# Halved projections, eight square buffers and kept weights in a Conformer convolution stage

## The chip, the cores and the metric

The kernel runs on one core of one Trainium2 chip. A core has a matrix engine (TensorE, PE in the profile, with its weight loads listed apart as PEld), VectorE (DVE), ScalarE (ACT), GpSimd (POOL) and SyncE (SP), whose queue issues nearly all DMA transfers here. Each engine works through its own queue in order; the order on each is fixed when the program is built. The metric is the device time of one launch in microseconds; smaller is better.

## The reference

One inference step of a small streaming encoder with 1024 channels: 640 frames in all, 512 of a new stream (the prompt) and 8 running streams with 16 new frames each (the sample). Layer 0 is a Conformer convolution module followed by a SwiGLU FFN, layer 1 is chunked attention with an FFN. Only the convolution module is touched:

```python
def conv_module(h, hist, g, w_pw1, b_pw1, w_dw, b_dw, ln_g, ln_b, w_pw2, b_pw2):
    a, gate = jnp.split(rms_norm(h, g) @ w_pw1 + b_pw1, 2, axis=-1)
    glu = a * jax.nn.sigmoid(gate)
    full = jnp.concatenate([hist.astype(glu.dtype), glu], axis=1)
    y = lax.conv_general_dilated(
        full, w_dw[:, None, :].astype(full.dtype), window_strides=(1,), padding="VALID",
        dimension_numbers=("NWC", "WIO", "NWC"), feature_group_count=D_MODEL) + b_dw
    y = jax.nn.silu(layer_norm(y, ln_g, ln_b))
    return h + y @ w_pw2 + b_pw2, full[:, -CONV_HIST:]
```

So: a norm, a projection to 2 x 1024 channels, a gate, a causal convolution over 31 frames in each channel, a layer norm over the channels of each frame, silu, and a second projection that is added to the residual. Everything is float32.

## The kernel before, in words

Channels lie on the 128 partitions, in 8 blocks (0 to 7); frames lie along the free dimension, in two groups of 320 (group 0: the 128 sample frames and 192 of the prompt; group 1: the other 320). A float32 product is made of three passes of a rounded format: weights and activations are split into a high and a low part (`whi`, `wlo`, `xh`, `xl`), and `mm3` (lines 164 to 166) issues hi*hi, lo*hi and hi*lo. `wsplit` loads a weight tile of 1 MB into `raw` (SP queue, line 133), ScalarE makes `whi` (line 144) and VectorE `wlo` (line 148); each of the three tags has two buffers, so a tile can be split only when the one two before it is done with.

The stage is written as a list of steps, PLAN, which `step` works through in that order. A scheduler with a model of each engine's time then fixes the order on each engine; the place in the program is the priority, and blocks marked `high_priority` are moved ahead. For channel block c the steps are:

- `a`, `b`, `c`, `C`: the first projection and gate of block c. One group (`glu_`) takes two products of 24 matmuls, each in its own PSUM buffer (tag `mm`, four buffers that go round); ScalarE reads the gate with a tanh (line 582) and the linear half (line 585) into t tiles, VectorE multiplies them into `gall`, the row of history and new frames (lines 589, 595). `C` does both groups and also prepares the convolution on TensorE: `conv_load` expands the taps into `w4` on GpSimd (line 641), `conv_shift` writes the row to DRAM (`sa` for the sample and group 0, `sb` for group 1, line 650) and reads it back four times shifted (`xa`, `xb`, two buffers each, line 656). `D` (not in the plan before) is `C` with a row of the sample frames alone.
- `S`, `A`, `B`: the convolution of block c on TensorE (`conv_pe`, line 674): sample frames, the prompt frames of group 0, group 1. They use PSUM buffers of the same tag `mm`, and ScalarE copies the result into `y` (line 602).
- `d`: the convolution on VectorE, tap by tap (`conv`, line 623); `dp1s0` is the prompt of block 1 and the sample of block 0, and so on. `q`: the prompt's convolution of a block on GpSimd: ScalarE multiplies a tap (`cvt`, line 633, four buffers), GpSimd adds it to `ca` (line 636), 31 times; at the end ScalarE copies `ca` to `y`.
- `L7`: the late read of block 7's `xb`. `s`: the convolution state goes out.
- `n0`, `n1`: `conv_ln`, the layer norm of a group. `colmean` sums over channels: the first `cut` pieces are added up on GpSimd (`acc`, line 190), and what is left goes to TensorE as matmuls with a single column of ones (line 199), one for each piece and each of three tiles of frames. The mean is spread over the partitions (line 211), VectorE subtracts it (line 688), ScalarE squares (line 171), the squares are summed likewise (`rstd_bc`), GpSimd takes the root's inverse (line 239), VectorE multiplies (line 694), ScalarE does silu (line 696) and the split follows (lines 153, 154).
- `w0`, `w1`: `pw2`, the second projection of a group, in four weight tiles `m2` (48 matmuls a tile and group); VectorE adds the result to `h` (line 714).

The FFN follows, on the same engines: it computes the statistics of the first 320 frames, then of the second, and its first matmuls (line 361) need the normalised first half. PSUM tiles of tag `w2` (two buffers) hold the statistics and VectorE's convolutions.

Of the kernel before, what the change touches and what calls it, by code (L numbers as in the profile page):

```python
# [15 lines left out]
P = 128  # L16
D = 1024
# [24 lines left out]
HP = 2000  # L42
CUT, LCUT = 8, 6
PO = {2: 0, 4: 1}
PL1 = (0, 2, 0, 0, 0, 0, 0, 0)
PL2 = (0, 0)
SQ = 'aaaaaaaa'
C01 = 4
# [24 lines left out]
def tile_trunk(ctx, tc, xT, vecs, hist, w_pw1, w_pw2, w_in0, w_out0, w_in1, w_out1,  # L73
# [93 lines left out]

    def square(s, n, eng="a"):
        q = tp.tile([P, tw[0]], F32, tag="sq", name=nm("sq"))
        if eng == "a":  # L170
            nc.scalar.activation(out=q[:, :n], in_=s, func=AF.Square)
# [54 lines left out]
    def rstd_bc(pieces, n, engs=SQ, cut=CUT, r2=None, eng=nc.gpsimd, newton=False,  # L226
                accp=None):
# [451 lines left out]
    def conv_ln(g):  # L679
        n = gr[g][1]  # L680
        mu = w2t()
        order = LNO[g]
        r, v = colmean(mu, [lambda c=c: y[g][:, c, :] for c in order], n, LCUT if g else 0, "mst")
        if v is not r:
            nc.vector.tensor_copy(r[:, :len(tiles(n))], v)
        spread(mu, r, n)
        for c in order:
            nc.vector.tensor_tensor(out=y[g][:, c, :], in0=y[g][:, c, :], in1=mu[:, :n],
                                    op=ALU.subtract)
        bc, _ = rstd_bc([y[g][:, c, :] for c in order], n, SQ, 1)  # L690
        z = new_xs(g)
        for c in range(KT):
            yc = y[g][:, c, :]
            nc.vector.tensor_tensor(out=yc, in0=yc, in1=bc, op=ALU.mult)
            s = tp.tile([P, tw[0]], F32, tag="n1", name=nm("n1"), bufs=NB1)
            nc.scalar.activation(out=s[:, :n], in_=yc, func=AF.Silu, scale=col(V_LNG, c),
                                 bias=col(V_LNB, c))
            xsplit(s[:, :n], z[0][:, c, :], z[1][:, c, :])
# [20 lines left out]
    def step(op, arg):  # L719
# [13 lines left out]
        elif op == "x":  # L733
            def mid():
                xs[1] = rms(1, V_NCONV, SSQ1, 8, hold=w4t)
            glu(1, 0, *pws[1], mid=mid)
        elif op in "DC":
            load_hist(c, c + 1)
            w4 = conv_load(c)
            pws[c + 1] = wsplit(w_pw1[c + 1] if c + 1 < KT else w_pw2[0], 16, P)  # L740
            glu_(c, 0, *pws[c], None)
            xa = conv_shift(c, "a", 0, NXA if op == "C" else NSC)
            nc.sync.dma_start(convs_out[:, c], gs[:, c])
            glu(c, 1, *pws[c])
            x4s[c] = w4, xa, op == "C" and conv_shift(c, "b", NSC + HA, NXB, c == KT - 1)
        elif op == "d":
# [3 lines left out]
        elif op == "L":  # L750
            x4s[c] = x4s[c][:2] + (x4s[c][2](),)
        elif op in "SAB":
# [451 lines left out]
```

## Time and profile before

| | before |
|---|---|
| time, median of 3 runs | 1572.77 us (1565.56 to 1572.9) |
| the profiled execution's own time | 1570.35 us |
| its span, first to last instruction | 1568.3 us |
| granted TensorE clock, mean | 0.971 |
| TensorE busy | 1503.2 us, 96% |
| VectorE, ScalarE, GpSimd busy | 1004.9, 674.7, 213.4 us |
| DMA | 164.30 MB, mean 105 GB/s |

The convolution stage takes the first 292 us of the span; the rest is FFN, attention, FFN. In the profile a line such as `L199 PE MATMUL w<-onec,sq` reads: line 199 of the kernel, engine, operation, output tile from input tiles. A timeline row begins with start and duration in us; consecutive rows of one kind are merged, and their number stands behind an x. A window row begins with the stretch, its length, and the busy time of each engine with the number of instructions. The chain of work that ended last is followed back from the last instruction, at each step to what released it.

### The profile page before, as it was taken

The numbers are of one execution on the slowest core, as the hardware profiler recorded it, in microseconds if no ns is written. First come the engines' busy times: TensorE is split into PE (matmuls) and PEld (weight loads), VectorE is DVE, ScalarE is ACT, GpSimd is POOL, SyncE is SP. The second block draws the span as 40 slices with busy tenths as digits, with TensorE's granted clock in tenths as the row PEclk, the third lists the DMA queues.
The fourth block names the chain that finished last, engine by engine and source line by source line (L and its number), as shares of the span: only waits on it lengthen the run. The fifth ranks groups of instructions, "written<-read, shape, count | busy, mean of one in ns | idle before, by whom it ended". The sixth has DMA issues, their size and how long they took to land.

```text
span 1568.3 us, 27283 instructions
## 1 busy us (share of the span) xinstructions
PE 1503.2 (96%) x11186; PEld 1428.8 (91%) x11186; DVE 1004.9 (64%) x1997; ACT 674.7 (43%) x1295; POOL 213.4 (14%) x239
## 2 busy tenths in 40 slices
PE   5999799999999999999999999988999999999997
PEld 5998579999999999999988788866999999999996
DVE  5788435785675575558676667563685575575555
ACT  4665145454254244246654344442444254244233
POOL 5789001000000000004221111011000000000001
PEclk9999679999999999999999999997999999999998
DMA  7256303312213222223555554351112222222211
GB/s 231 72 150 174 82 20 108 135 48 88 81 61 101 81 74 88 82 81 114 194 179 169 170 182 165 125 196 57 55 48 88 81 70 92 81 74 88 81 54 68
DMA packets 55884, 164.30 MB, mean 105 GB/s; under 512 B 10064, under 2 KB 24528, under 8 KB 47056
## 3 DMA queue, kind: packets, MB, share of 16 engines
q1 hardware_dynamic: 55472, 162.26, 32.2%
q8 instruction: 88, 1.44, 0.4%
q10 hardware_dynamic: 288, 0.31, 0.1%
q14 instruction: 36, 0.29, 0.1%
HBM read 151.13 MB, written 11.42 MB: 104 GB/s over the span
## 4 chain that ended last, share of the span: by engine, by line
PE 83%; POOL 5%; DVE 4%; ACT 3%; DMA 2%; issue 2%; POOLq 0%; SPq 0%; DVEq 0%; ACTq 0%
PE mm L361 35%; PE mm L164 13%; PE mm L166 12%; PE mm L165 12%; POOL ca L636 5%; PE w L199 2%; PE mm L674 2%; PE w L1001 1%; PE am L986 1%; PE am L1032 1%; PE am L969 1%; DMA cache<-in_ck 1%; ACT whi L144 1%; PE w L945 1%; PE w L946 1%
## 5 line engine op out<-in xcount | busy, mean ns | idle before, releaser
L361 PE MATMUL mm<-XH,wlo 128*128 128x320 f32 x736 | 228.3, 311 | 0.4 <-DVE wlo L319 0.4
L361 PE MATMUL mm<-XH,whi 128*128 128x320 f32 x736 | 227.4, 311 | 0.0
L361 PE MATMUL mm<-XL,whi 128*128 128x320 f32 x736 | 225.4, 309 | 0.0
L164 PE MATMUL mm<-xh,whi 128*128 128x320 f32 (+2 forms) x640 | 203.2, 320 | 5.9 <-ACT xh L153 4.2
L165 PE MATMUL mm<-xh,wlo 128*128 128x320 f32 (+2 forms) x640 | 202.0, 316 | 0.6 <-DVE wlo L148 0.6
L166 PE MATMUL mm<-xl,whi 128*128 128x320 f32 (+2 forms) x640 | 199.8, 316 | 0.0
L165 PE MATMUL mm<-hid,wlo 128*128 128x320 f32 (+2 forms) x560 | 171.8, 308 | 0.0
L166 PE MATMUL mm<-hid,whi 128*128 128x320 f32 (+2 forms) x560 | 169.7, 308 | 0.0
L164 PE MATMUL mm<-hid,whi 128*128 128x320 f32 (+2 forms) x560 | 167.7, 308 | 0.0
L318 ACT ACTIVATE whi<-raw 128x1536 fp32r<-128x1536 f32 (+2 forms) x90 | 101.0, 1148 | 121.3 <-PE mm L166 89.2
L319 DVE TENSOR_TENSOR wlo<-raw,whi 128x1536 fp32r<-128x1536 f32 (+2 forms) x90 | 118.7, 1340 | 40.6 <-ACT whi L318 40.4
L361 PEld LDWEIGHTS mm<-XH,wlo 128*128 128x128 f32 x736 | 139.2, 189 | 0.8 <-DVE wlo L319 0.8
L361 PEld LDWEIGHTS mm<-XH,whi 128*128 128x128 f32 x736 | 138.8, 189 | 0.0
L361 PEld LDWEIGHTS mm<-XL,whi 128*128 128x128 f32 x736 | 137.9, 188 | 0.0
L164 PEld LDWEIGHTS mm<-xh,whi 128*128 128x128 f32 x640 | 123.3, 193 | 9.9 <-ACT xh L153 4.9
L165 PEld LDWEIGHTS mm<-xh,wlo 128*128 128x128 f32 x640 | 123.6, 193 | 1.2 <-DVE wlo L148 0.8
L166 PEld LDWEIGHTS mm<-xl,whi 128*128 128x128 f32 x640 | 123.2, 194 | 1.2 <-issue 1.0
L361 PE MATMUL mm<-XH,vhi 128*128 128x320 f32 x368 | 114.2, 310 | 1.9 <-ACT XH L445 1.9
L361 PE MATMUL mm<-XH,vlo 128*128 128x320 f32 x368 | 113.8, 309 | 0.0
L361 PE MATMUL mm<-XL,vhi 128*128 128x320 f32 x368 | 113.1, 308 | 0.2
L165 PEld LDWEIGHTS mm<-hid,wlo 128*128 128x128 f32 x560 | 105.1, 188 | 0.0
L166 PEld LDWEIGHTS mm<-hid,whi 128*128 128x128 f32 x560 | 104.7, 188 | 0.0
(210 smaller groups left out, 3404.4 us busy)
## 6 DMA issues: line engine op xcount, KB each, us to landing
raw<-in_w_in SPq DMA_DIRECT2D x38, 1024.0 KB
cache<-in_ck SPq DMA_DIRECT2D x32, 512.0 KB
cache<-in_cv SPq DMA_DIRECT2D x32, 512.0 KB
raw<-in_w_pw SPq DMA_DIRECT2D x14, 1024.0 KB
raw<-in_w_out SPq DMA_DIRECT2D x18, 768.0 KB
raw<-in_w_kq SPq DMA_DIRECT2D x8, 1024.0 KB
raw<-in_w_in SPq DMA_DIRECT2D x12, 512.0 KB
raw<-in_w_out SPq DMA_DIRECT2D x12, 384.0 KB
```

The source lines that it names most:

```text
L144: nc.scalar.activation(out=hi[:, a:b], in_=raw[:, a:b], func=AF.Copy)
L164: nc.tensor.matmul(ps, wh, xh, start=(i == 0), stop=False)
L165: nc.tensor.matmul(ps, wl, xh, start=False, stop=False)
L166: nc.tensor.matmul(ps, wh, xl, start=False, stop=(i == last))
L199: nc.tensor.matmul(st[:, 512 + t * w + k:513 + t * w + k], s[:, a:a + P], onec, start=True, stop=True)
L318: nc.scalar.activation(out=hi[:, a:b], in_=src, func=AF.Copy)
L319: nc.vector.tensor_tensor(out=lo[:, a:b], in0=src, in1=hi[:, a:b].bitcast(F32), op=ALU.subtract)
L361: nc.tensor.matmul(pt, wt, v[x][:, k, :], start=(first and k == i == 0), stop=(k == 3 and i == 2), skip_group_check=True)
L636: nc.gpsimd.tensor_tensor(out=acc, in0=acc, in1=pr, op=ALU.add)
L674: nc.tensor.matmul(pt[32 * q:32 * q + 32, 0:n], w4[0:r, 4 * tg + q, :], mv, start=(tg == 0), stop=(tg == 7))
L945: nc.tensor.matmul(ps, QQ[:, q], KK[:, 0:n], start=True, stop=False)
L946: nc.tensor.matmul(ps, QQ[:, q], KL[:, 0:n], start=False, stop=True)
```

## The change

The plan is rewritten, and four smaller things are changed.

1. Steps `E` and `F` are new: `E` is the group 0 half of `C` (history, taps, next weights, products, the `sa`/`xa` transfers), `F` the group 1 half (products, `sb`/`xb`). Blocks 6 and 7 use them, with convolutions between: `E6 S4 A4 F6 B4 E7 S5 A5 F7 S6 A6`, where before stood `S4 A4 B4 C6 S5 A5 C7 S6 A6`.
2. Block 3 uses `D`, so its sample convolution is on TensorE (`S3`); VectorE's last convolution is `ds2` instead of `ds2s3`.
3. Group 0's mean has its first five pieces added on GpSimd (before: none), group 1's five (before six), in other orders. The squares are written to a tile with eight places, at the place of the low part of group 1's activations, where before two buffers went round. Group 1's squares are all added on GpSimd (before: none), group 0's none, as before.
4. The multiply, silu and split of group 0 have high priority, and silu writes to the four `cvt` buffers where before it had two of its own.
5. The second projection of group 1 takes the weight tiles in the order 2, 3, 0, 1 and uses tiles 2 and 3 as group 0 left them, without loading and splitting them again.

```diff
-CUT, LCUT = 8, 6
+CUT, LCUT, SQCUT = 8, (5, 5), (1, 8)
...
+M2 = ((0, 1, 2, 3), (2, 3, 0, 1))
...
-LNO = ((0, 1, 4, 2, 5, 3, 6, 7), (0, 1, 4, 2, 5, 3, 6, 7))
-PLAN = ("a0 y x1 b0 b1 q0 dp1s0 c2 ds1p2 c3 C4 q3 ds2s3 C5 S4 A4 B4 C6 S5 A5 C7 S6 A6 S7 A7 n0 B5 L7 B6 "
-        "B7 s0 n1 w0 w1")
+LNO = ((0, 1, 4, 5, 6, 2, 3, 7), (0, 1, 4, 2, 3, 5, 6, 7))
+PLAN = ("a0 y x1 b0 b1 q0 dp1s0 c2 ds1p2 D3 C4 S3 q3 ds2 C5 E6 S4 A4 F6 B4 E7 S5 A5 F7 S6 A6 S7 "
+        "A7 n0 B5 L7 B6 B7 s0 n1 w0 w1")
...
-    def square(s, n, eng="a"):
-        q = tp.tile([P, tw[0]], F32, tag="sq", name=nm("sq"))
+    def square(s, n, eng="a", q=None):
+        if q is None:
+            q = tp.tile([P, tw[0]], F32, tag="sq", name=nm("sq"))
...
-        r, v = colmean(st, [lambda s=s, e=e: square(s, n, e) for s, e in zip(pieces, engs)], n,
+        r, v = colmean(st, [lambda s=s, e=e, i=i: square(s, n, e, sqs if sqs is None else sqs[:, i, :])
+                         for i, (s, e) in enumerate(zip(pieces, engs))], n,
                        cut, "rst", eng, accp)
...
-        r, v = colmean(mu, [lambda c=c: y[g][:, c, :] for c in order], n, LCUT if g else 0, "mst")
+        r, v = colmean(mu, [lambda c=c: y[g][:, c, :] for c in order], n, LCUT[g], "mst")
...
-        bc, _ = rstd_bc([y[g][:, c, :] for c in order], n, SQ, 1)
+        sq = xp.tile([P, KT, n], F32, tag="xl1", name=nm("sql"))
+        bc, _ = rstd_bc([y[g][:, c, :] for c in order], n, SQ, SQCUT[g], sqs=sq)
         z = new_xs(g)
-        for c in range(KT):
...
-            s = tp.tile([P, tw[0]], F32, tag="n1", name=nm("n1"), bufs=NB1)
...
+        with tc.high_priority(offset=HP * (1 - g)):
+            for c in range(KT):
...
+                s = cp.tile([P, T], F32, tag="cvt", name=nm("cvt"), bufs=CVT)[:, :n]
...
     def pw2(g, z):
         n = gr[g][1]
-        for m2 in range(KT // 2):
-            if g == m2 == 0:
-                wh, wl = pws[KT]
-            else:
-                wh, wl = wsplit(w_pw2[m2], 16, P, pool=PL2[g])
+        for m2 in M2[g]:
+            if (KT, m2) not in pws:
+                pws[KT, m2] = wsplit(w_pw2[m2], 16, P, pool=PL2[g])
+            wh, wl = pws[KT, m2]
+            if m2 < 2:
+                del pws[KT, m2]
...
-        elif op in "DC":
-            load_hist(c, c + 1)
-            w4 = conv_load(c)
-            pws[c + 1] = wsplit(w_pw1[c + 1] if c + 1 < KT else w_pw2[0], 16, P)
-            glu_(c, 0, *pws[c], None)
-            xa = conv_shift(c, "a", 0, NXA if op == "C" else NSC)
-            nc.sync.dma_start(convs_out[:, c], gs[:, c])
-            glu(c, 1, *pws[c])
-            x4s[c] = w4, xa, op == "C" and conv_shift(c, "b", NSC + HA, NXB, c == KT - 1)
+        elif op in "CDEF":
+            if op != "F":
+                load_hist(c, c + 1)
+                w4 = conv_load(c)
+                if c + 1 < KT:
+                    pws[c + 1] = wsplit(w_pw1[c + 1], 16, P)
+                else:
+                    pws[KT, 0] = wsplit(w_pw2[0], 16, P)
+                glu_(c, 0, *pws[c], None)
+                x4s[c] = [w4, conv_shift(c, "a", 0, NSC if op == "D" else NXA), None]
+                nc.sync.dma_start(convs_out[:, c], gs[:, c])
+            if op != "E":
+                glu(c, 1, *pws[c])
+                if op != "D":
+                    x4s[c][2] = conv_shift(c, "b", NSC + HA, NXB, c == KT - 1)
```

More of the change, by code (lines that the diff above doesn't have):

```diff
@@ L226, in rstd_bc @@
     def rstd_bc(pieces, n, engs=SQ, cut=CUT, r2=None, eng=nc.gpsimd, newton=False,
-                accp=None):
+                accp=None, sqs=None):
         st = w2t()
         nt = len(tiles(n))
-        r, v = colmean(st, [lambda s=s, e=e: square(s, n, e) for s, e in zip(pieces, engs)], n,
+        r, v = colmean(st, [lambda s=s, e=e, i=i: square(s, n, e, sqs if sqs is None else sqs[:, i, :])
+                         for i, (s, e) in enumerate(zip(pieces, engs))], n,
                        cut, "rst", eng, accp)
@@ L689, in conv_ln @@
                                     op=ALU.subtract)
-        bc, _ = rstd_bc([y[g][:, c, :] for c in order], n, SQ, 1)
+        sq = xp.tile([P, KT, n], F32, tag="xl1", name=nm("sql"))
+        bc, _ = rstd_bc([y[g][:, c, :] for c in order], n, SQ, SQCUT[g], sqs=sq)
         z = new_xs(g)
-        for c in range(KT):
-            yc = y[g][:, c, :]
-            nc.vector.tensor_tensor(out=yc, in0=yc, in1=bc, op=ALU.mult)
-            s = tp.tile([P, tw[0]], F32, tag="n1", name=nm("n1"), bufs=NB1)
-            nc.scalar.activation(out=s[:, :n], in_=yc, func=AF.Silu, scale=col(V_LNG, c),
-                                 bias=col(V_LNB, c))
-            xsplit(s[:, :n], z[0][:, c, :], z[1][:, c, :])
+        with tc.high_priority(offset=HP * (1 - g)):
+            for c in range(KT):
+                yc = y[g][:, c, :]
+                nc.vector.tensor_tensor(out=yc, in0=yc, in1=bc, op=ALU.mult)
+                s = cp.tile([P, T], F32, tag="cvt", name=nm("cvt"), bufs=CVT)[:, :n]
+                nc.scalar.activation(out=s, in_=yc, func=AF.Silu, scale=col(V_LNG, c),
+                                     bias=col(V_LNB, c))
+                xsplit(s, z[0][:, c, :], z[1][:, c, :])
         return z
@@ L750, in step @@
         elif op == "L":
-            x4s[c] = x4s[c][:2] + (x4s[c][2](),)
+            x4s[c][2] = x4s[c][2]()
         elif op in "SAB":
```

## The prediction

> **What bounds the kernel now.** I read the page first, then the chain of work that ended last, then windows of busy time around the one place where the clock row dips, then the timelines of TensorE, ScalarE, VectorE and GpSimd there.
>
> ```profile
> PE 1503.2 (96%) x11186; PEld 1428.8 (91%) x11186; DVE 1004.9 (64%) x1997; ACT 674.7 (43%) x1295; POOL 213.4 (14%) x239
> ...
> PEclk9999679999999999999999999997999999999998
> ```
>
> TensorE is busy 96% of the span, so only its idle time, its slow time and its useless work can be saved. The clock row has one deep dip, slices 5 and 6 (157 to 235 us): the end of the convolutions and the layer norms. The windows of that stretch (columns: PE, PEld, DVE, ACT, POOL busy with counts, granted clock, DMA share, GB/s):
>
> ```profile
> 155.50:161.20 5.70, 4.82 (x129) 3.71 (x128) 3.79 (x12) 4.22 (x8) 1.41 (x2) 1.00 0.49 192
> 161.20:178.30 17.10, 6.73 (x128) 5.25 (x128) 12.46 (x31) 1.36 (x5) 0.00 (x0) 0.70 0.81 150
> 178.30:195.00 16.70, 16.66 (x103) 11.11 (x103) 0.35 (x2) 0.00 (x0) 0.00 (x0) 0.59 0.00 1
> 195.00:216.90 21.90, 20.38 (x223) 13.98 (x222) 6.04 (x18) 8.07 (x16) 2.59 (x3) 1.00 0.15 35
> 216.90:239.30 22.40, 21.69 (x92) 21.43 (x93) 8.68 (x20) 9.87 (x22) 0.00 (x0) 0.54 0.00 1
> 239.30:292.40 53.10, 53.10 (x372) 52.93 (x370) 34.45 (x49) 29.63 (x42) 8.04 (x7) 1.00 0.41 140
> 292.40:301.10 8.70, 5.83 (x31) 5.31 (x30) 8.56 (x16) 5.64 (x9) 0.00 (x0) 0.80 0.41 130
> ```
>
> Two kinds of loss: 10.4 us idle in the second window (17.10 - 6.73), and 56 us at a clock of 0.54 to 0.70. The chain names the idle:
>
> ```profile
> 157.22 0.45 ACT y L602
> 157.67 0.42 ACT t L582
> ...
> 158.88 2.73 DMA sa<-gall
> ...
> 162.99 6.49 DMA xa<-sa
> 169.94 6.73 PE mm L674 x128
> 176.67 1.67 issue
> ```
>
> The tanh of channel block 7 (t) runs only at 157.67, behind y<-ca, the end of GpSimd's convolution q3; from it a round trip through DRAM takes until 162.99 + 6.49 = 169.48, and S7, A7 start then. The slow time comes from the statistics, matmuls that stream one column (L199). Prices at both clocks, from TensorE's timeline (an fp32 matmul of these shows as two records; start, us, count):
>
> ```profile
> 109.67 4.56 PE L674 MATMUL mm<-xa,w 128*32 128x128 f32 x128
> 114.05 4.50 PE L674 MATMUL mm<-xb,w 128*32 128x320 f32 x64
> ...
> 155.55 1.96 PE L674 MATMUL mm<-xa,w 128*32 128x128 f32 x64
> ...
> 183.01 6.56 PE L199 MATMUL w<-onec,y 128*128 128x1 f32 x30
> ...
> 199.20 1.50 PE L199 MATMUL w<-onec,sq 128*128 128x1 f32 x12
> ...
> 219.04 4.00 PE L199 MATMUL w<-onec,sq 128*128 128x1 f32 x18 [0.66 <-ACT sq L171]
> ```
>
> and of the chain, the products:
>
> ```profile
> 223.52 0.27 PE mm L164
> ...
> 309.24 66.73 PE mm L361 x455
> ```
>
> So a statistics record costs 0.125 us warm (1.50/12) and 0.22 us at half clock (6.56/30, 4.00/18); a product matmul 0.147 us warm (66.73/455; the same 128x320 shape) and 0.27 at half clock; S+A 4.56, B 4.50, S alone 1.96 us warm.
>
> **The change part by part.**
>
> *E/F halves.* Before, C6, S5 A5, C7, S6 A6 stood between; now E7, S5 A5, F7, S6 A6. Behind E7's products TensorE has S5 A5 4.56 + F7's 48 x 0.147 = 7.0 + S6 A6 4.56 = 16.2 us of work, before 11.6. The trip from t to landed xa took 169.48 - 157.67 = 11.8 us, which fits if t runs at once. It won't: ScalarE's queue is paced by GpSimd (y<-ca waits 4.02 us for it; below, the two timelines).
>
> ```profile
> 152.37 0.55 ACT L585 ACTIVATE t<-mm,hb 128x320 f32<-128x320 f32 x1
> 156.94 0.72 ACT L602 ACTIVATE y<-ca 128x192 f32<-128x192 f32 x2 [4.02 <-POOL ca L636]
> 157.58 0.51 ACT L582 ACTIVATE t<-mm,hb 128x320 f32<-128x320 f32 x1
> ```
>
> ```profile
> 130.07 1.92 POOL L641 TENSOR_TENSOR w<-i,dwv 128x1024 f32<-128x1024 f32 x1
> ```
>
> In the written order E7's second product comes earlier by S5 A5 (4.6) and later by the new S3 (2.0): 2.6 us. Its neighbour, the linear half (L585, at 152.37, one product or 3.5 us earlier), already stands ahead of y<-ca, so t most likely moves ahead too, to about 152.4, plus 1.9 us because q3 gets one more tap expansion (L641: D3 uses a third early buffer) on GpSimd. xa then lands at 154.3 + 11.8 = 166; TensorE reaches S7 at 161 + 2.0 + 1.5 (stalls, below) = 164.5. The wait is 0 to 9 us; I take 3: **-6**. With a short wait the clock holds and S7 A7 take 4.56 instead of 6.73: **-2**.
>
> *What each moved step issues.* E6/E7 issue history, taps, the next weights, the sa/xa transfers and convs; F6/F7 sb/xb. SP is in order: xb6 waits for B4 (buffer), xa7 for A5, and the next raw weights stand behind; by the order above both are done some 5 and 10 us before SP gets there. In PSUM (four buffers) F6/F7 now want E6's and E7's banks after S, A and one product (4.6 + 3.5 = 8.1 us), where before A5 wanted C6's second bank after 7.0 + 1.96 = 9.0 us and stalled 0.70:
>
> ```profile
> 137.18 2.81 PE L674 MATMUL mm<-xa,w 128*32 128x192 f32 x64 [0.70 <-ACT t L582]
> ```
>
> Three such places, each at worst as late as t is now: 0 to 6, **+1.5**.
>
> *D3, S3, ds2.* S3 adds 64 records to TensorE, **+2**. VectorE loses 31 of its 62 sample taps, which run till 174.6:
>
> ```profile
> 167.97 6.62 DVE L623 SCALAR_TENSOR_TENSOR w<-gall,dwv,w 128x128 f32<-128x128 f32 x17
> ```
>
> They held y[0][2] and y[0][3], and with them part of the 1.67 us gap behind A7: **-1** (0 to -1.7).
>
> *Statistics.* The windows of that line alone:
>
> ```profile
> 178.30:195.00 16.70, 8.73 (x48) 8.56 (x48) 0.59 0.00 1
> ...
> 216.90:239.30 22.40, 9.10 (x42) 9.37 (x42) 0.54 0.00 1
> ```
>
> Group 0's mean: 8 pieces x 3 tiles = 48 records become 24 (four adds on GpSimd, in front of the last pieces 2, 3, 7): 8.7 us at half clock become 3.0 warm or 5.3 slow, **-5**. Group 1's mean: cut 6 to 5, 18 to 24 records, **+0.7**.
>
> *B5 in the slow stretch.* The 54 conv records of 178 to 195 us took 16.7 - 8.7 = 8.0 us; warm they are 54 x 0.070 = 3.8. If the clock holds -4.2, else 0: **-3.5**.
>
> *Squares.* Group 0 keeps 48 records. Group 1 had those 42 of 216.9 to 239.3 and 6 behind; now 6 in all, since GpSimd adds all eight: **-9**. The other 50 records of that window are products, 42 of them slow: 42 x 0.12 = **-5** when nothing sparse stands between them, and the 0.66 us idle goes, **-0.7**. These products stayed slow although TensorE was busy 21.69 of 22.40 us, and the clock rose at 239.3, behind the last block but one of statistics: I take the sparse blocks for the cause. The Trainium skill, TensorE: Matmul & The Clock Gate, Part 1, has the clock halved after an idle window of about 3.4 us and full again after one busy window of that length. If every busy record counts as activity there, the products should have been warm by about 224, and this -5 would be some -1, a time of 1552; the trace disagrees, unless one-column matmuls don't count.
>
> *What is late next.* Group 1's chain: squares, seven GpSimd adds, z. The groups of 216.95 to 292.5 us (count, busy, mean ns, idle before), and an add of the window before:
>
> ```profile
> L148 DVE TENSOR_TENSOR wlo<-raw,whi 128x2048 fp32r<-128x2048 f32 x6 | 13.7, 2291 | 6.5 <-ACT whi L144 6.4
> ...
> L144 ACT ACTIVATE whi<-raw 128x2048 fp32r<-128x2048 f32 x6 | 11.4, 1904 | 6.2 <-PE mm L166 6.2
> ...
> L696 ACT ACTIVATE n<-y,vec 128x320 f32<-128x320 f32 x14 | 9.0, 646 | 6.0 <-DVE xl L154 3.3 <-DVE y L694 2.8
> ...
> L153 ACT ACTIVATE xh<-n 128x320 fp32r<-128x320 f32 x15 | 6.9, 463 | 0.3
> ...
> L190 POOL TENSOR_TENSOR acc<-acc,sq 128x320 f32<-128x320 f32 x4 | 5.3, 1317 | 2.2 <-ACT sq L171 2.0
> ...
> L171 ACT ACTIVATE sq<-y 128x320 f32<-128x320 f32 x8 | 3.7, 466 | 8.1 <-PE w L199 6.8 <-DVE y L688 1.3
> ...
> L239 POOL TENSOR_TENSOR rst<-rst,mhalf 128x3 f32<-128x3 f32 x2 | 1.9, 946 | 32.6 <-DVE rst L232 32.6
> ```
>
> ```profile
> L190 POOL TENSOR_TENSOR acc<-acc,y 128x320 f32<-128x320 f32 x3 | 2.6, 869 | 41.0 <-ACT y L602 40.9
> ```
>
> z of group 0 now goes first on ScalarE, 8 x (0.65 + 0.46) = 8.9 us, then 3.7 of squares; the adds, 7 x 1.32 = 9.2 at worst, run beside them and end a little later: some 13.5 us after the second projection begins. Root and spread about 3, then z of group 1, 9 us alone and 16 with weight splits between: ready 25 to 32 us in. Group 0's products cover 192 x 0.147 = 28.2, and the last piece is needed 3 us later. A stall of 0 to 4, **+2**.
>
> *Kept weights.* Two loads fewer, 2 x 1.9 us of ScalarE and 2 x 2.3 of VectorE, in a window where TensorE is busy 53.10 of 53.10: nothing. But group 1 now ends on rows 0 to 3, which the FFN's second-half squares add first, so three or four links follow the last row; ScalarE and VectorE carry them while they build the FFN's first operands, for which TensorE already idles 2.9 of 8.7 us (the last window): 0 to 4, **+1.5**. Eight square buffers, four silu buffers and the priority of z cost nothing by themselves; the squares' tile is that of xs[1], last read by F7, 9 us of convolutions earlier.
>
> Sum: -6 -2 +1.5 +2 -1 -5 +0.7 -3.5 -9 -5 -0.7 +2 +1.5 = -24.5. Against the profiled execution, 1570.35, that is 1545.9; the median of the runs, 1572.77, is 2.4 above it, so I say 1548. With every term at its good end it is about -35 (1538), with every one at its bad end +3 (1575).
>
> **The rivals.**
>
> *A: t stays behind y<-ca* (the halves don't do what they are for). The order moves by 2.6 us, the margin between its neighbour and itself was 3.5, so this is close. Then the 9 us wait, the slow S7 A7 and B5 stay (6 + 2 + 3.5 back): -13, **1560**.
>
> *B: the stretch only trades waits*: A, and besides group 1's chain at its bad end (+2 more), the PSUM places and the FFN's start at theirs (+4.5 and +2.5): -4, **1569**, no change. For it: ScalarE and GpSimd are in order and paced by q3. Against: ScalarE is busy only 9.87 of 22.40 us in the squares' window.
>
> *D: the slow clock isn't the statistics' doing.* The products of group 0 begin at half clock, after the sparse stretch ahead of them, and stay so some 20 us as in the window of 0.54: the -5 is lost, **1553**. For it: TensorE was nearly full there and still slow. Against: from 239.3 on it is warm with the same products.
>
> *C: slower.* SP's in-order queue: a raw weight tile stuck behind an xa or xb read that waits for a convolution.
>
> ```profile
> 5.26 6.81 DMA raw<-in_w_pw
> ```
>
> A tile that is late by its whole path (landing as here, then the split) costs 6.8 + 1.9 + 2.3 = 11 us. Three of them (blocks 6 and 7, then the first of the second projection) turn -24.5 into +8.5, **1581**; two still leave a gain. Block 7's tile is asked for 23 us (F6 7.0, E6 7.0, S4 A4 4.6, B4 4.5) before E7 wants it, so its issue must slip 12 us.
>
> **How the numbers follow.** Forecast 0.60, D 0.08, A 0.14, B 0.07, C 0.11. No change means within 0.5% (7.9 us: 1564.9 to 1580.6), about what a measurement of this kernel can tell. Faster: the forecast, D and nearly all of A, 0.81; same: B and a rest of A, 0.08; slower: C, 0.11. The range goes from a little under the good ends to beyond A, 1535 to 1565; the forecast's own range is 1537 to 1557.
>
> **What would show it.** Right: S7 A7 within 4 us of A6; L199 records of group 0's mean 24, of group 1's squares 6; no half-clock products inside the second projection's first 20 us; its end 20 to 30 us earlier; two L133 loads fewer. Wrong: t of block 7 still after y<-ca; TensorE idle between the projection's groups or waiting for wlo L148 in E6, E7; a longer gap ahead of the first L361.

## The result, and the profile after

The changed kernel takes 1543.38 us (median of 4 runs, 1540.99 to 1553.67) against 1569.16 us for the kernel before (median of 4, 1554.33 to 1572.9), 25.8 us less: a ratio of 0.9887, with a 95% interval of 0.984 to 0.9934. In a second comparison on one chip (f1 below) the medians are 1545.87 and 1563.85 us, 18.0 us apart: 0.989 (0.9863 to 0.9917). The prediction was 1548 us, range 1535 to 1565.

The profiled execution took 1543.31 us (span 1541.4, mean granted clock 0.986), against 1570.35 us before. The page, first two rows as shown of before:

```profile
PE 1480.1 (96%) x11190; PEld 1409.6 (91%) x11190; DVE 994.1 (64%) x1963; ACT 668.7 (43%) x1293; POOL 229.8 (15%) x250
...
PEclk9999899999999999999999999999899999999998
```

TensorE executes four instructions more and is busy 23.1 us less: 64 short records of S3 came in, 60 of the statistics' went out, and fewer of the others run at a low clock. The dip of the clock row (before 6 and 7 in slices 5 and 6) is down to one 8. The windows of the same stretch (columns: PE, PEld, DVE, ACT, POOL busy with counts, clock, DMA share, GB/s), then the second projection as one window, after and before:

```profile
155.00:167.20 12.20, 6.02 (x139) 5.01 (x137) 8.50 (x17) 4.77 (x10) 4.16 (x4) 0.88 0.70 164
167.20:174.00 6.80, 6.77 (x132) 6.03 (x132) 0.00 (x0) 0.62 (x2) 0.00 (x0) 0.71 0.84 146
174.00:198.00 24.00, 24.00 (x232) 15.72 (x236) 5.32 (x14) 5.74 (x13) 4.32 (x5) 0.86 0.15 35
...
262.00:276.00 14.00, 8.69 (x47) 7.87 (x46) 11.77 (x20) 7.02 (x12) 0.00 (x0) 0.88 0.31 92
```

```profile
203.60:266.40 62.80, 62.01 (x434) 61.67 (x433) 34.55 (x58) 29.07 (x50) 18.78 (x14) 1.00 0.28 96
```

```profile
217.00:292.40 75.40, 74.74 (x462) 74.32 (x462) 43.03 (x69) 39.40 (x63) 8.04 (x7) 0.86 0.29 99
```

Idle is still in the first row (12.20 - 6.02 = 6.2 us) and in the last (5.3 us). The projection runs at full clock and with 28 records fewer.

Six marks cut the time. The first `hid` is the first matmul of the first FFN's second projection, which reads the tile `hid`.

| mark, us from the span's start | before | after | length before | length after | difference |
|---|---|---|---|---|---|
| A6 ends | 160.95 | 161.02 | | | +0.1 |
| S7 A7 end | 176.67 | 173.68 | 15.7 | 12.7 | -3.1 |
| second projection begins | 216.95 | 203.60 | 40.3 | 29.9 | -10.4 |
| second projection ends | 292.5 | 266.6 | 75.5 | 63.0 | -12.5 |
| first `hid` | 375.8 | 352.2 | 83.3 | 85.6 | +2.3 |
| end of the execution | 1570.35 | 1543.31 | 1194.5 | 1191.1 | -3.4 |

By the first `hid` 23.6 us are gained. The last 3.4 us lie in code that the change doesn't touch; two executions of one kernel differ by more.

What still holds S7 back is in the timelines of ScalarE, VectorE and SP's queue of the changed kernel (start, duration; in brackets idle before and what ended it):

```profile
151.43 0.83 ACT L605 ACTIVATE y<-w 128x128 f32<-128x128 f32 x3 [4.65 <-DVE w L626]
152.13 0.54 ACT L585 ACTIVATE t<-mm,hb 128x320 f32<-128x320 f32 x1
155.11 0.72 ACT L605 ACTIVATE y<-ca 128x192 f32<-128x192 f32 x2 [2.43 <-POOL ca L639]
```

```profile
147.27 6.74 DVE L626 SCALAR_TENSOR_TENSOR w<-gall,dwv,w 128x128 f32<-128x128 f32 x18
153.92 1.31 DVE L592 SCALAR_TENSOR_TENSOR gall<-t,t 128x128 f32<-128x128 f32 x1
```

```profile
156.21 0.32 SPq L653 DMA_DIRECT2D sa<-gall  x1
159.22 1.85 SPq L659 DMA_DIRECT2D xa<-sa  x4
```

The tanh of block 7 (L585, now the gate's line) did move ahead of `y<-ca`, from 157.67 to 152.13. But it stands behind `y<-w`, which waited 4.65 us for VectorE's taps, and its product into `gall` waits for 18 of those taps until 153.92. Of 5.5 us gained on ScalarE only 2.7 are left where `sa` is written (158.88 before, 156.21 after).

The chain of work that ended last shows the norms in their new order: the statistics (L201) follow A7 without a gap, and behind the 48 squares stand 44 convolution records.

```profile
164.80 2.34 POOL acc L192
167.23 6.45 PE mm L677 x128
173.69 2.32 PE w L201 x20
...
184.27 6.68 PE w L201 x48
190.94 5.41 PE mm L677 x44
```

The first row has to be read with care: the profile names a GpSimd add as what released S7, but S7 reads `xa` and the taps and nothing of `acc`. In all eight other profiles with the same plan, that of the same program (f1) among them, the wait is named `DMA xa<-sa`, and in two of them (e1, f4) no add of GpSimd lies within the 7 us ahead of S7; I read it as the transfer here too. Finally the waits of TensorE in this stretch; nearly all the idle time has two names, S7's wait and the FFN's start (L364). The last row is the one wait inside the second projection:

```profile
PE mm L677 <- POOL acc L192: 6.2, 1, 6.2
PE mm L364 <- ACT XH L448: 4.0, 1, 4.0
PE mm L364 <- DVE XL L449: 1.3, 1, 1.3
...
PE w L201 <- POOL acc L192: 0.8, 1, 0.8
```

### The profile page after: what moved, and what is told of

Its sections match the earlier page's. It is cut to its first block, busy times and chain, and to the rows that moved or that the text cites. A ratio compares the mean times of both kernels' runs of the same rounds, so it can differ in the third digit from the quotient of the medians.

```text
span 1541.4 us, 27271 instructions
## 1 busy us (share of the span) xinstructions
PE 1480.1 (96%) x11190; PEld 1409.6 (91%) x11190; DVE 994.1 (64%) x1963; ACT 668.7 (43%) x1293; POOL 229.8 (15%) x250
## 4 chain that ended last, share of the span: by engine, by line
PE 84%; POOL 5%; DVE 5%; DMA 2%; ACT 2%; issue 2%; POOLq 0%; DVEq 0%; ACTq 0%
PE mm L364 36%; PE mm L165 13%; PE mm L166 12%; PE mm L167 12%; POOL ca L639 4%; PE mm L677 2%; DMA cache<-in_ck 1%; PE w L201 1%; PE w L1013 1%; PE am L998 1%; PE am L981 1%; PE am L1044 1%; DVE w L626 1%; ACT whi L145 1%; PE w L957 1%
## 5 line engine op out<-in xcount | busy, mean ns | idle before, releaser
L364 PE MATMUL mm<-XH,wlo 128*128 128x320 f32 x736 | 228.9, 311 | 0.5 <-DVE wlo L322 0.5
L364 PE MATMUL mm<-XH,whi 128*128 128x320 f32 x736 | 227.9, 312 | 0.0
L364 PE MATMUL mm<-XL,whi 128*128 128x320 f32 x736 | 225.9, 310 | 0.0
L364 PEld LDWEIGHTS mm<-XH,wlo 128*128 128x128 f32 x736 | 139.5, 190 | 1.2 <-DVE wlo L322 1.2
L364 PEld LDWEIGHTS mm<-XH,whi 128*128 128x128 f32 x736 | 139.4, 190 | 0.0
L364 PEld LDWEIGHTS mm<-XL,whi 128*128 128x128 f32 x736 | 138.3, 189 | 0.0
L364 PE MATMUL mm<-XH,vhi 128*128 128x320 f32 x368 | 115.4, 314 | 4.0 <-ACT XH L448 4.0
L364 PE MATMUL mm<-XL,vhi 128*128 128x320 f32 x368 | 114.5, 312 | 1.4 <-DVE XL L449 1.3
L364 PE MATMUL mm<-XH,vlo 128*128 128x320 f32 x368 | 115.3, 313 | 0.0
```

The lines of the kernel that those rows point to most:

```text
L364: nc.tensor.matmul(pt, wt, v[x][:, k, :], start=(first and k == i == 0), stop=(k == 3 and i == 2), skip_group_check=True)
```

## The experiments

From e1 on each kernel ran beside the kernel before, on the same chip, and those that name the same time of before ran together; e5 ran once. The marks are those of one profile each. Diffs are against the changed kernel. "Behind A7" is the time from A7's end to the end of the second projection.

| run | median us | before beside it | ratio, 95% interval | S7's wait | A7 ends | behind A7 | first `hid` |
|---|---|---|---|---|---|---|---|
| before | 1569.16 | | | 9.0 | 176.67 | 115.8 | 375.8 |
| after | 1543.38 | 1569.16 | 0.9887 (0.984 to 0.9934) | 6.2 | 173.7 | 92.9 | 352.2 |
| e1 plan only | 1554.18 | 1563.13 | 0.9943 (0.9913 to 0.9973) | 7.5 | 176.7 | 105.8 | 365.3 |
| e2 norms only | 1552.91 | 1563.13 | 0.994 (0.9913 to 0.9967) | 9.3 | 174.6 | 100.6 | 361.6 |
| e3 nothing kept | 1548.32 | 1563.13 | 0.9913 (0.9887 to 0.9939) | 5.7 | 172.4 | 96.7 | 353.5 |
| e4 FFN order | 1545.21 | 1563.13 | 0.9888 (0.9849 to 0.9927) | 5.7 | 171.7 | 96.1 | 351.1 |
| e5 one tap | 1542.68 | 1561.33 | one run | 1.9 | 169.7 | 92.9 | 346.6 |
| e6 squares on TensorE | 1553.03 | 1561.33 | 0.9951 (0.9922 to 0.998) | 6.4 | 172.5 | 101.2 | 362.1 |
| e7 S2 on TensorE | 1555.99 | 1561.33 | 0.9973 (0.9943 to 1.0003) | 7.2 | 186.2 | 92.9 | 363.0 |
| e8 ds2 later | 1547.99 | 1561.33 | 0.9924 (0.9894 to 0.9954) | 7.4 | 173.8 | 92.9 | 350.7 |
| f1 after again | 1545.87 | 1563.85 | 0.989 (0.9863 to 0.9917) | 6.3 | 173.3 | 96.2 | 355.2 |
| f2 FFN order again | 1542.02 | 1563.85 | 0.9861 (0.9832 to 0.989) | 5.8 | 171.8 | 96.1 | 351.2 |
| f3 halves undone | 1551.07 | 1563.85 | 0.9911 (0.9877 to 0.9945) | 10.2 | 178.2 | 92.9 | 356.8 |
| f4 mean on TensorE | 1548.32 | 1563.85 | 0.9901 (0.9868 to 0.9935) | 3.9 | 172.7 | 96.1 | 355.9 |

**e1, the plan alone**, with the norms, their buffers and the weights as before:

```diff
-CUT, LCUT, SQCUT = 8, (5, 5), (1, 8)
+CUT, LCUT, SQCUT = 8, (0, 6), (1, 1)
...
-M2 = ((0, 1, 2, 3), (2, 3, 0, 1))
+M2 = ((0, 1, 2, 3), (0, 1, 2, 3))
...
-LNO = ((0, 1, 4, 5, 6, 2, 3, 7), (0, 1, 4, 2, 3, 5, 6, 7))
+LNO = ((0, 1, 4, 2, 5, 3, 6, 7), (0, 1, 4, 2, 5, 3, 6, 7))
...
-        sq = xp.tile([P, KT, n], F32, tag="xl1", name=nm("sql"))
-        bc, _ = rstd_bc([y[g][:, c, :] for c in order], n, SQ, SQCUT[g], sqs=sq)
+        bc, _ = rstd_bc([y[g][:, c, :] for c in order], n, SQ, SQCUT[g])
...
-        with tc.high_priority(offset=HP * (1 - g)):
+        if True:
...
-                s = cp.tile([P, T], F32, tag="cvt", name=nm("cvt"), bufs=CVT)[:, :n]
+                s = tp.tile([P, tw[0]], F32, tag="n1", name=nm("n1"), bufs=NB1)[:, :n]
...
-            if m2 < 2:
-                del pws[KT, m2]
+            del pws[KT, m2]
```

> The changed kernel's plan (D3, S3, ds2, E and F halves) with everything else as before. Marks used in all runs: start of the second projection (before 217.0, changed 203.6 us) and the first matmul of the first FFN's output product (before 375.8, changed 352.2 us). My theory, that the gain is the sum of nearly separate terms: S7 A7 end about 173.7 as in the changed kernel (-3), the mean of group 0 keeps 48 records (+5 against the changed kernel), so the second projection starts near 208 to 210; the 48 square records and the half-clock products stay in it, so the FFN mark is near 367 (-9). Rival, that the halves are what pays: FFN mark 360 or less. Rival, that the plan alone gives nothing: 374 to 377.

**e2, the norms alone**, with the plan and the weights as before:

```diff
-M2 = ((0, 1, 2, 3), (2, 3, 0, 1))
+M2 = ((0, 1, 2, 3), (0, 1, 2, 3))
...
-PLAN = ("a0 y x1 b0 b1 q0 dp1s0 c2 ds1p2 D3 C4 S3 q3 ds2 C5 E6 S4 A4 F6 B4 E7 S5 A5 F7 S6 A6 S7 "
-        "A7 n0 B5 L7 B6 B7 s0 n1 w0 w1")
+PLAN = ("a0 y x1 b0 b1 q0 dp1s0 c2 ds1p2 c3 C4 q3 ds2s3 C5 S4 A4 B4 C6 S5 A5 C7 S6 A6 S7 A7 n0 B5 L7 B6 "
+        "B7 s0 n1 w0 w1")
...
-            if m2 < 2:
-                del pws[KT, m2]
+            del pws[KT, m2]
```

> The old plan and weights loaded for both groups; only the norms are changed (eight square buffers, GpSimd sums, priority and buffers of silu). My theory: the wait for xa stays 9 us and S7 A7 end at 176.7; the mean saves about 5, the squares and the warm products 12 to 14, so the FFN mark is near 358 (-17). Rival, that the halves are needed for the norms to pay (old order keeps the clock low): 365 or more.

By the first `hid` the plan alone gains 10.5 us, the norms alone 14.2 (2.1 of them are there at A7's end, ahead of the norms). That makes 24.7, against 23.6 together, closer than single profiles can tell: the parts add up, and the norms don't need the halves. That the plan's gain lies where the prediction put it is not borne out by e1: A7 ends where it ended before (176.7). `sa` did go out 3.4 us sooner than before (158.88), but from there to S7's start it took 14.3 us, against 11.1 before and 11.0 in the changed kernel, so the round trip took that gain away; why it was longer is open.

```profile
155.49 0.32 SPq L653 DMA_DIRECT2D sa<-gall  x1
159.74 2.65 SPq L659 DMA_DIRECT2D xa<-sa  x4
```

The 10 us of e1 come behind A7. Of these 6.3 lie ahead of the second projection: the gap behind A7 is gone, and the mean's 48 records take 6.0 us for 8.7. The other 3.8 lie in it: the rows of e1 show it cold for 5 us only, though the one-column blocks are still there, 12 records at a time (the first window and a later one, then one of the blocks):

```profile
210.70:215.70 5.00, 5.00 (x19) 5.00 (x20) 2.96 (x9) 3.46 (x8) 0.00 (x0) 0.50 0.00 0
...
225.70:230.70 5.00, 5.00 (x41) 5.00 (x39) 2.79 (x3) 2.23 (x3) 0.00 (x0) 1.00 0.13 20
```

```profile
226.02 1.39 PE L201 MATMUL w<-onec,sq 128*128 128x1 f32 x12
```

Before, one of the same blocks, cold, and a window with it:

```profile
227.32 2.55 PE L199 MATMUL w<-onec,sq 128*128 128x1 f32 x12
```

```profile
227.00:232.00 5.00, 5.00 (x22) 5.00 (x22) 0.98 (x2) 2.43 (x5) 0.00 (x0) 0.50 0.00 0
```

The same 12 records between products, 2.9 us of products up to the next block in e1 and 4.0 before, leave a warm TensorE warm and go along with a cold one that stays cold (the three windows from 222 to 237 us all have 0.50).

**e3, the weights not kept**: the order 0 to 3 for both groups, all tiles loaded.

```diff
-M2 = ((0, 1, 2, 3), (2, 3, 0, 1))
+M2 = ((0, 1, 2, 3), (0, 1, 2, 3))
...
-            if m2 < 2:
-                del pws[KT, m2]
+            del pws[KT, m2]
```

> The changed kernel with group 1's weights loaded again, in the order 0 to 3. My theory: the two loads are hidden, and the order 2, 3, 0, 1 costs at the FFN's start, so the FFN mark is 2 to 4 us earlier than the changed kernel's (348 to 350) and the idle time before the first FFN products is 3 us instead of 5.3. Rival, that the kept tiles pay: 354 or more, with waits for whi or wlo inside the second projection.

The mark came 1.3 us later. From the projection's end to the mark e3 took 84.5 us, the changed kernel 85.6: the order does cost there, by 1.1 us, less than I thought. The stretch behind A7 is 3.8 us longer, but 3.3 of that lie ahead of the projection, where the weights play no part (a slow spell of the clock, see the last section); the projection itself took 63.4 us against 63.0. So the kept tiles are worth about 0.4 us here, and nothing tells the time from the changed kernel's.

**e4 and f2, the order of the FFN's squares**: the rows with which group 1's projection ends now also come last in the sum over the second half.

```diff
-            bc, _ = rstd_bc([h[:, k, sl] for k in range(KT)], NH, SQ, 6, None,
+            ks = (4, 5, 6, 7, 0, 1, 2, 3) if half and not l else range(KT)
+            bc, _ = rstd_bc([h[:, k, sl] for k in ks], NH, SQ, 6, None,
```

> The changed kernel; only the first FFN's second-half squares are added in the order 4, 5, 6, 7, 0, 1 with 2, 3 on TensorE, which is the order in which the kept weights finish the rows. My theory (three or four links behind the last row): the FFN mark moves 2 to 4 us ahead, to 348 to 350, and the half-clock run of FFN products at 283.8 to 287 goes. Rival, that the gap is the memory or the normalisation of the first half: 352 unchanged.

> The changed kernel itself, beside the next three on one chip. If it is the time of this kernel and not chance that the runs so far showed, its ratio to the kernel before comes out at 0.984 to 0.993 again. If the full clock with which its second projection began at 203.6 us was luck of phase, this profile may begin that projection at 0.63 to 0.69 of full clock, as other variants did, and end it some 3 us later.

> The order of the FFN's squares, against the changed kernel on the same chip. By the marks it saves 2.3 us up to the first out-product and 4.1 up to the first with vhi; if that carries to the end, the median lies 2 to 4 us under the changed kernel's beside it (0.13% to 0.26%, at the edge of what five rounds tell). If the FFN's later stages take it up, the two are within 1 us.

The waits at the FFN's start in f2, which stand for the 4.0 and 1.3 us of the changed kernel:

```profile
PE w L201 <- ACT sq L173: 1.2, 1, 1.2
...
PE mm L364 <- DVE XL L450: 1.0, 1, 1.0
...
PE mm L364 <- DVE wlo L322: 0.3, 1, 0.3
PE mm L364 <- ACT XH L449: 0.3, 1, 0.3
```

In both runs the first `hid` came 83.3 us after the projection's end, against 85.6 in both profiles of the changed kernel; the first `vhi` 4 us sooner. That names the cause of the longer FFN start: the adds behind the last row. In the first comparison the medians didn't show it (0.9888 against 0.9887). On one chip, with six runs each, f2 is at 1542.02 (1539.76 to 1545.82) and the changed kernel at 1545.87 (1543.34 to 1551.39), 3.9 us apart, as expected. The intervals of the two ratios overlap; f2 is the fastest kernel here by its median. By the marks the order gives 2.3 us of that up to the first `hid`, in both runs.

**e5, one tap**: of the 31 taps that `ds2` adds on VectorE only the first is done.

```diff
-        for j in range(W):
+        for j in range(1 if items == [(2, 0)] else W):
```

> The changed kernel with 30 of the 31 taps of block 2's sample convolution on VectorE (ds2) left out, so that VectorE's queue ahead of block 7's gate is free. My theory: block 7's tanh (152.1) and gate products (153.9 to 156.2) stand behind ds2 on ScalarE and VectorE, so sa goes out 3 to 4 us earlier, and TensorE's wait in front of S7 falls from 6.2 us to 1 to 3; the second projection starts 4 to 6 us earlier (198 to 200). Rival 1, that GpSimd's q3 is what holds the tanh: the wait stays 5 to 6. Rival 2, that the add of the mean on GpSimd, which the trace names as the releaser, holds S7: the wait stays 6 whatever xa does.

The tanh ran at 150.45, and S7 waited 1.9 us:

```profile
150.45 0.55 ACT L585 ACTIVATE t<-mm,hb 128x320 f32<-128x320 f32 x1
```

```profile
152.97 0.34 SPq L653 DMA_DIRECT2D sa<-gall  x1
157.18 1.74 SPq L659 DMA_DIRECT2D xa<-sa  x4
```

```profile
165.11 4.58 PE L677 MATMUL mm<-xa,w 128*32 128x128 f32 x128 [1.94 <-DMA xa<-sa]
```

`y<-ca` is as late as ever (156.22), so GpSimd's convolution is not what holds the tanh after the change; VectorE's taps are. `sa` goes out 3.2 us sooner than in the changed kernel, but its reads only 2.0, and S7 starts 2.1 us sooner. The other half of the shorter wait is no gain: A6 ends 2.2 us later, since TensorE waits 2.8 us for ScalarE's `y` ahead of A5. A7 ends 4.0 us sooner, 2.1 by the transfer and 1.9 because S7 and A7 run at the warm price. At the mark it is 5.6 us, 1.6 of them in the FFN's start.

**e6, group 1's squares on TensorE** as before:

```diff
-CUT, LCUT, SQCUT = 8, (5, 5), (1, 8)
+CUT, LCUT, SQCUT = 8, (5, 5), (1, 1)
```

> The changed kernel with group 1's squares summed on TensorE again (48 records instead of 6), all else as changed. By the prediction's terms: 42 records x 0.12 to 0.2 = 5 to 8 us, and 5 more if the sparse blocks hold the clock down; minus the 2 us that the late adds cost: FFN mark 357 to 363. Rival (the clock isn't the statistics' doing): products between the blocks are warm after the first 5 us and the cost is 4 to 6 us alone, FFN mark 356 to 358.

The second projection took 71.3 us against 63.0: +8.3, of which 1.6 lie in its first 16 products and the 6 records behind them, where nothing was changed but the clock is lower. The mark is 9.9 us later, as expected. One block of 36 records shows the clock's part, TensorE busy all the time:

```profile
217.49 4.89 PE L201 MATMUL w<-onec,sql 128*128 128x1 f32 x36
```

```profile
217.50:222.50 5.00, 5.00 (x38) 5.00 (x38) 0.64 (x2) 0.00 (x0) 0.00 (x0) 0.80 0.61 213
222.50:227.50 5.00, 5.00 (x20) 5.00 (x21) 0.26 (x2) 0.00 (x0) 0.85 (x1) 0.51 0.00 0
227.50:232.50 5.00, 5.00 (x38) 5.00 (x37) 3.75 (x10) 4.30 (x6) 0.00 (x0) 1.00 0.00 0
```

After the 4.89 us of one-column matmuls the products run at 0.51 for 5 us and are warm again in the window after.

**e7, S2 on TensorE too**, to free VectorE from `ds2`:

```diff
-PLAN = ("a0 y x1 b0 b1 q0 dp1s0 c2 ds1p2 D3 C4 S3 q3 ds2 C5 E6 S4 A4 F6 B4 E7 S5 A5 F7 S6 A6 S7 "
+PLAN = ("a0 y x1 b0 b1 q0 dp1s0 D2 ds1p2 D3 S2 C4 S3 q3 C5 E6 S4 A4 F6 B4 E7 S5 A5 F7 S6 A6 S7 "
...
+                if c not in pws:
+                    pws[c] = wsplit(w_pw1[c], 16, P)
```

> The changed kernel with block 2's sample convolution on TensorE too (D2, S2 instead of c2, ds2). TensorE gets 2.0 us more, VectorE loses 31 taps. If ds2 is what holds block 7's gate: wait in front of S7 1 to 3 us instead of 6.2, FFN mark 349 to 351. If q3 holds it: wait 5 to 6, mark 353 to 355.

**e8, ds2 later in the list**, behind E7:

```diff
-PLAN = ("a0 y x1 b0 b1 q0 dp1s0 c2 ds1p2 D3 C4 S3 q3 ds2 C5 E6 S4 A4 F6 B4 E7 S5 A5 F7 S6 A6 S7 "
+PLAN = ("a0 y x1 b0 b1 q0 dp1s0 c2 ds1p2 D3 C4 S3 q3 C5 E6 S4 A4 F6 B4 E7 ds2 S5 A5 F7 S6 A6 S7 "
```

> The changed kernel with ds2 behind E7 in the list, so at a lower priority than block 7's gate. If VectorE's queue ahead of the gate is the cause: wait in front of S7 1 to 4 us; but ds2 may then end later than A7 and hold the mean of group 0 (needed at 173): FFN mark 348 to 354. If q3 is the cause: wait 5 to 6 and the mark 353 or later.

Neither recovers what e5 showed. In e7 A7 ends 12.5 us later than in the changed kernel: TensorE has 2.0 us more work, it waits 4.3 us for `whi` and 2.6 for `wlo` at 56 to 61 us (0.6 for `wlo` in the changed kernel), and the tanh of block 7 now waits for TensorE itself; what lies behind A7 is the same 92.9 us. In e8 ScalarE still waits 4.64 us for the taps ahead of the tanh: the scheduler put them in the same place, so the run doesn't test a later `ds2`, and its time is that of the changed kernel within the intervals.

**f3, the halves undone**, D3, S3 and all of the norms kept:

```diff
-PLAN = ("a0 y x1 b0 b1 q0 dp1s0 c2 ds1p2 D3 C4 S3 q3 ds2 C5 E6 S4 A4 F6 B4 E7 S5 A5 F7 S6 A6 S7 "
+PLAN = ("a0 y x1 b0 b1 q0 dp1s0 c2 ds1p2 D3 C4 S3 q3 ds2 C5 S4 A4 B4 C6 S5 A5 C7 S6 A6 S7 "
```

> The changed kernel with C6 and C7 whole again (D3, S3 and the single ds2 stay, and all of the norms). Theory: t of block 7 stands behind VectorE's taps wherever the halves are, and what the halves give is TensorE's work behind t, 4.6 us more of it: so S7 waits 9 to 11 us instead of 6.2, S7 and A7 still run slow at 6.5 to 6.7 us, and everything behind is 3 to 5 us later, about 1547 to 1549. Rival: the halves give nothing, since C7's first product also comes earlier by S3 and S5 moved away: wait and time within 1.5 us of the changed kernel. Second rival: the halves gave all the 6 us I forecast and more and the rest of the list costs: over 6 us later.

S7 waited 10.2 us, S7 and A7 took 6.89 (slow, a little over the 6.5 to 6.7), and A7 ended 4.9 us later than in f1 beside it. The medians differ by 5.2 us, 1551.07 being above the expected 1547 to 1549, and their intervals overlap. Not all of the 4.9 us is the tanh's: `sa` goes out 2.2 us later than in f1, and from its write to the issue of its reads it takes 5.1 us for 2.5. My theory's reason was off: here the tanh runs at 156.13, behind `y<-ca` again, as before the change.

```profile
155.09 0.72 ACT L605 ACTIVATE y<-ca 128x192 f32<-128x192 f32 x2 [5.64 <-POOL ca L639]
...
156.13 0.52 ACT L585 ACTIVATE t<-mm,hb 128x320 f32<-128x320 f32 x1
```

```profile
171.35 6.89 PE L677 MATMUL mm<-xa,w 128*32 128x128 f32 x128 [10.22 <-DMA xa<-sa]
```

So it is the halves that bring the tanh ahead of `y<-ca`, as the prediction had it, and f3 is its rival A, built.

**f4, group 0's mean on TensorE** as before (48 records, not 24):

```diff
-CUT, LCUT, SQCUT = 8, (5, 5), (1, 8)
+CUT, LCUT, SQCUT = 8, (0, 5), (1, 8)
```

> The changed kernel with group 0's mean summed by TensorE alone, 48 records instead of 24. Theory: the records themselves are what costs, 24 more at 0.125 warm to 0.22 slow, so the second projection begins 3.0 to 5.3 us later and the marks behind it too, with a time of 1546 to 1549. Rival: the adds on GpSimd only shift the wait, because the mean's root of the chain is the last pieces of y either way: within 1.5 us of the changed kernel. Second rival: more records keep the clock down over B5 and the products, as rival D has it the other way round: over 6 us later.

The 48 records took 5.75 us, warm (0.12 each), where the 24 take 0.83 + 1.70 + 0.61 = 3.1. The projection begins 31.8 us after A7, against 29.9 to 30.0 in eight profiles with 24 records and 33.2 in two (e3, f1), and ends 96.1 us after it, against 92.9 to 96.2 where the weights are kept and the squares added on GpSimd. The expected 3.0 to 5.3 us isn't there: 2.6 us of records, and what reaches the end is within the spread of the clock. The median, 1548.32, lies in the expected range, 2.4 us over f1's and inside the intervals.

## Why the prediction was right, point by point

The forecast of -24.5 us was the sum of five stretches; here are the terms against the marks. That the sums agree to 1 us is in part luck: misses in opposite directions cancel, the marks are of one profile each, and the medians differ by 25.8 us in the first comparison and by 18.0 in the second.

| stretch | terms | forecast | measured |
|---|---|---|---|
| to A6's end | PSUM stalls +1.5, S3 +2 | +3.5 | +0.1 |
| to A7's end | xa wait -6, S7 A7 warm -2 | -8 | -3.1 |
| to the second projection | ds2 gap -1, means -5 and +0.7, B5 -3.5 | -8.8 | -10.4 |
| second projection | squares -9, products -5, 0.66 idle -0.7, chain +2 | -12.7 | -12.5 |
| to the first `hid` | FFN order +1.5 | +1.5 | +2.3 |
| sum | | -24.5 | -23.6 |

**xa's wait: the step that failed, hidden by the one before it.** The prediction said that t would move ahead of `y<-ca`, and run at about 152.4 plus 1.9; it ran at 152.13, and f3 shows that without the halves it doesn't move. But I had priced its queue on ScalarE by GpSimd alone. The taps of `ds2`, which I counted only for the gap behind A7, stand on VectorE ahead of the product that follows the tanh, and on ScalarE through `y<-w`: `sa` went out 4.1 us after the tanh, before 1.2. In e5, without the taps, it goes out 3.2 us sooner. The two errors happened to cancel, t 2.2 us sooner than forecast and `sa` 2.9 us later behind it: S7 was to start at 164.5 + 3 = 167.5 and started at 167.23. TensorE, however, was there at 161.02 and not at 164.5, so it waited 6.2 us and not 3, and behind that wait S7 and A7 stayed slow (6.45 us for my 4.56). So of the two terms it is the -2 that cost time; in e5 they took 4.58 us behind 1.9 us of idle time.

**PSUM stalls and S3.** S3's 64 records came (1.96 us in their row), but the stretch got no longer. In the windows of 95 to 161 us TensorE was busy 62.67 us before and 64.03 after:

```profile
95.00:161.00 66.00, 62.67 (x741) 55.86 (x739) 57.79 (x126) 40.56 (x67) 55.20 (x39) 1.00 0.68 180
```

```profile
95.00:161.00 66.00, 64.03 (x805) 57.55 (x803) 60.52 (x123) 37.84 (x64) 56.85 (x40) 1.00 0.68 181
```

The idle time went from 3.3 to 2.0 us, so the stalls, whose bounds I had put at 0 to 6, were -1.4. I had excluded a gain there without a reason; S3 may itself be work that covers a wait, which no run shows. Nor is the base firm: in e2, which has the plan of before, A6 ends at 158.5, 2.4 us sooner than in before, for a reason that stays open. A6 of f3, whose plan differs from e2's by D3, S3 and the single `ds2` alone, ends 2.6 us later than e2's, about what I had put for S3. The two misses (3.4 us better, 4.9 worse) belong together, since a TensorE that comes sooner waits longer for the same transfer; they leave the start of the norms 1.5 us behind the forecast.

**Means, gap and B5.** The stretch was forecast to 1.6 us. Up to the spread of group 0's mean it is 12.0 us shorter, where gap, mean and B5 were to give 9.5. The gap behind A7 is gone whole (1.67 us, I took 1). The mean fell from 8.7 to 3.1 us: f4 shows 2.6 us for the records; the other 3.0 are the clock, as my two prices had it. What is left for B5 is 4.7 (I took 3.5). Behind that point the stretch is 1.7 us longer, where I had put +0.7: the 48 squares now stand in one block, the clock falls in it, and the 44 convolution records behind it take 0.12 us each for 0.07 warm.

**The second projection.** Squares and the products slowed by them: forecast -9 and -5; putting the squares back into the changed kernel costs 8.3 (e6) for both, since most of its products stay warm. The chain of group 1 was late by 0.8 us, the wait for GpSimd's last add that is all the idle time of the 62.80 us, so +2 was 0.8, and the -14.7 of the other terms came out 1.4 smaller.

**The half clock (-5, and rival D against it).** Half right. The sparse blocks are a cause: in e6 the clock falls inside one, 3 us after its start, although TensorE was warm and busy, and in the changed kernel and f1 it falls inside the block of 48 squares (188.4 and 187.8 us, last section). But e1 has blocks of 1.39 us that don't do this, and the projection of f2 turns cold at its start where the changed kernel, with the same records in the same order, stays at 1.00:

```profile
201.80:206.80 5.00, 5.00 (x25) 5.00 (x26) 2.01 (x6) 1.97 (x5) 0.00 (x0) 0.61 0.02 3
```

Nor did the projection of before begin at half clock, as rival D has it: its first 8 products ran at 1.00, and the clock fell in the 0.66 us wait behind them.

```profile
216.90:218.40 1.50, 1.43 (x8) 1.17 (x8) 1.50 (x4) 0.36 (x2) 0.00 (x0) 1.00 0.00 0
218.40:219.10 0.70, 0.06 (x1) 0.06 (x1) 0.70 (x3) 0.58 (x2) 0.00 (x0) 0.80 0.00 0
```

Ahead of them stood 5 us of statistics (210.4 to 215.4 us) and 1.57 us of idle time. So the 20 slow us of before go back in part to the sparse stretch ahead of the projection, which rival D named, and were kept slow by the blocks inside it, which I named; the share of each is not shown. The Trainium skill, TensorE: Matmul & The Clock Gate, Part 1, halves the clock after an idle window of about 3.4 us and restores it after a busy one of that length. The runs agree with the order of its length for products (in e1 and e6 a cold window of 5 us, then 1.00). They disagree with its rule if every busy record counts as activity: in e6 TensorE was busy for all of the 10 us in which its clock fell to 0.51. One-column matmuls that don't count, the exception that the prediction named, would explain it; no run has them alone.

**FFN order.** +2.3 for +1.5, by the mechanism named: f2 has none of it (83.3).

**The rivals.** A was built as f3: +4.9 us at A7's end where I had put +8 (6 and 2), since the wait and the clock were mostly not gained in the first place, and nothing behind A7 where I had put 3.5. B and C didn't come: SP's queue made nothing late in the changed kernel (TensorE's one wait for `wlo` up to S7 is 0.6 us at 53 us, and the kernel before has it too).

## What to carry to other kernels

When an instruction is to move ahead, follow its result over every engine up to the transfer that it feeds: here GpSimd's queue gave way on ScalarE, and VectorE's taps held the next step. Take the one-column matmuls of statistics off TensorE where another engine is idle; here they cost their own time and, in a long block, that of the products behind. And a list whose last row changes moves the sum behind it: order what sums over it likewise.

## What the runs showed of the hardware that was not expected

From A7's end to the projection's end TensorE hardly idles (0.8 us in the changed kernel), and with the changed norms and the kept weights the stretch took one of two lengths: 92.9 us (after, e5, e7, e8, f3) or 96.0 to 96.2 (e4, f1, f2). The 3.2 us are some 6 us more at half clock, and they fall in different places. Behind A7 the changed kernel has one slow spell, in group 0's squares and the convolution behind them (first row); f1 has two (second and third row):

```profile
188.40:196.00 7.60, 7.60 (x56) 4.38 (x56) 0.35 (x2) 0.12 (x1) 0.86 (x1) 0.56 0.01 2
```

```profile
177.70:181.00 3.30, 3.30 (x28) 1.25 (x20) 0.26 (x1) 0.00 (x0) 0.24 (x1) 0.52 0.02 5
...
187.80:197.60 9.80, 9.80 (x58) 7.51 (x61) 0.35 (x2) 0.00 (x0) 0.86 (x1) 0.50 0.04 8
```

f2 has three (175.8 to 179, 189.6 to 192.6 and 203 to 209.4 us); the last is the projection's start, shown above. f1 and the changed kernel are one program, so two of its executions can lie 3.2 us apart by this alone. What decides it was not tried.

VectorE's product of two SBUF tiles takes longer beside an add on GpSimd. In the changed kernel the product for the sample frames takes 1.31 us (the row is above) and lies beside an add of q3; the next, 1.03 us, beside another add; each ends 0.1 to 0.2 us behind its add. In f3 GpSimd has nothing to do at that point. The adds of the changed kernel, then the two products of f3:

```profile
153.78 1.30 POOL L639 TENSOR_TENSOR ca<-ca,cvt 128x512 f32<-128x512 f32 x1
155.04 0.93 POOL L192 TENSOR_TENSOR acc<-acc,y 128x320 f32<-128x320 f32 x1
```

```profile
157.42 0.28 DVE L592 SCALAR_TENSOR_TENSOR gall<-t,t 128x128 f32<-128x128 f32 x1
157.62 0.35 DVE L598 SCALAR_TENSOR_TENSOR gall<-t,t 128x192 f32<-128x192 f32 x1
```

That is 1.7 of the 4.1 us between the tanh and `sa`. The Trainium skill, GPSIMD Engine Reference, 1. Specifications, names the SBUF interfaces that the two engines share and the contention with VectorE instructions of two SBUF inputs; the rows agree and give its price here, 1.31 us for 0.28 and 1.03 for 0.35.

The write of `sa` and the issue of its reads lay 2.4 (f4), 3.0 (after), 4.2 (e1, e5) and 5.1 us (f3) apart, for the same bytes; what set it stays open, and the difference is as large as most terms of the sum.
